# Two products with one weight block in one 512-column matmul, summed when PSUM is read

## The chip, the cores and the metric

The kernel runs on one core of one Trainium2 chip. The metric is the device time of one execution in microseconds (us); three executions of the kernel before were timed. TensorE (PE in the profile, PEld for its weight loads) multiplies, VectorE (DVE) and ScalarE (ACT) do the elementwise work, GpSimd (POOL) sets constants, and SyncE (SP) issues all the large DMAs.

## The reference

Two layers of a diffusion backbone on 256 latent tokens and 256 context tokens of width 1024, in float32:

```python
x = x + 0.5 * m[2] * swiglu(modulate(x, norm_g[l, 0], m[0], m[1]), ffn1_wi[l], ffn1_wo[l])
# even layer: window attention with sink | bidirectional gated linear attention
y = jnp.concatenate([o_a, gla_output(o_b, rb, gla_g)], axis=-1) @ w_out
# odd layer: multi-scale pooling mixer
# then, in both, a second half-step SwiGLU
def swiglu(h, wi, wo):
    a, u = jnp.split(h @ wi, 2, axis=-1)
    return (jax.nn.silu(a) * u) @ wo
```

D_FF is 2816, so a down projection (`@ wo`) contracts 22 blocks of 128 into 8 blocks of 128 output columns; the mixer's output (`@ w_out`) contracts 8 blocks into 8. The context stream is needed only up to the first layer's mixer. The output is the latent stream after a last RMSNorm.

## The kernel before, in words

Activations lie with the features on partitions and the 256 tokens along the free dimension. A product keeps float32 precision by three matmuls: both operands are split into a high part (rounded to the type fp32r) and a low part (what rounding left), and high times high, high times low and low times high are summed in PSUM. The weights of a product come in by DMA as `raw`; ACT rounds them to `hi` (L142) and DVE subtracts to get `lo` (L143), in `weight` (L136). Each of `raw`, `hi` and `lo` has four buffers.

The program has these stages, with their place in the profiled span:

- the first SwiGLU for both streams (to 402 us), whose down projection runs twice with 512 columns, that is with both streams side by side;
- the mixer of the even layer (402 to 569 us), whose pieces of work are ordered by a planner (`Flow`, L61) with costs written by hand; its output projection is `output` (L925), in four groups of two output blocks (`OUT_N`), contraction blocks in the order `OUT_K`;
- the second SwiGLU, one stream (569 to 760 us, called ffn1 below), the third (760 to 950, ffn2), the pooling mixer (950 to 972) and the fourth (972 to the end, ffn3).

A SwiGLU stage (`ffn`, L337) first makes 22 pairs of up products (`product`, L303: 258 columns, of which 256 are tokens and two carry the shift); silu and the multiplication give a block of G, which `parts` (L328) splits into `G[0]` (ACT, L329) and `G[1]` (DVE, L330), two tiles. Then, for each of 8 output blocks n, 22 contraction blocks times three matmuls (L418 to L420) fill one PSUM bank, 256 columns wide for one stream. One DVE instruction (L430, called the eviction here) multiplies the bank by the gate and adds it to the residual stream, and `nxt.block` prepares the next stage's operand: a scaled copy by ACT (L299), its low part by DVE (L300), a square by ACT (L273) and a sum by DVE (L274). `Final.block` (L1083) does the like for the last norm.

DVE also makes the modulation vectors, 1024 elements at a time (L172, "dots" below), in a number per output block set by `RATES0` to `RATES3`: 1.2 in ffn1, 2 in ffn2, none in ffn3. Their weights (`rawm`, two buffers) share SP's queue with the stage's own weights. The order of each engine's instructions is fixed when the program is built, by a scheduler with its own estimates; engines then wait for one another by semaphores, each in its own order.

The mixer's output has the same three matmuls (L935 to L937) on the tile O, `[128, 2, 8, 258]`, whose second dimension is the part, and the same eviction (L951), two after each group.

Of the kernel before, what the change touches and what calls it, by code (L numbers as in the profile page):

```python
# [16 lines left out]
T = 256  # L17
# [43 lines left out]
class Flow:  # L61
    """Orders pieces of work so that TensorE always has one whose operands are there.

    A piece is a generator that emits instructions and yields step(...) with the time that they
    take on TensorE, what the other engines then do one after the other, the events that the
    next step needs and those that this one sets."""
# [34 lines left out]
def step(pe=0.0, post=(), needs=(), sets=()):  # L101
    return pe, post, needs, sets


class Body:
# [57 lines left out]
    def mod_dot(self, w, l, ch, k, s):  # L163
        """One block of adaLN's columns: a row of w_mod per partition times silu(c), plus its bias.
        Chunks 2 and 8 gate a half step and are halved here."""
# [19 lines left out]
    def step_mod(self, dots):  # L185
        """Spends `dots` of VectorE's time on the modulation and loads ahead for the next step."""
        self.credit += dots
        while self.units and self.credit >= len(self.units[0][3]):
            self.credit -= self.next_unit()
        while len(self.loaded) < min(2, len(self.units)):  # L190
            self.loaded.append(self.mod_load(*self.units[len(self.loaded)][:3]))
# [38 lines left out]
    def rstd_tables(self, sss, pool, tag, spare=None):  # L230
        """1/rms by the scalar engine's Ln and Exp and one Newton step, all streams at once."""
# [22 lines left out]
    def token_stats(self, ss):  # L254
        """Mean squares with the tokens on partitions, for rsqrt on a few columns."""
# [55 lines left out]

    def narrow(self, ps, w, X):
        """Product with 32 columns: a quarter of the contraction on each 32 columns of the array, and so
        four partial sums on 128 partitions."""
# [8 lines left out]
    def swiglu(self, out, za, zu, ba, bu):  # L323
        """out = silu(za + ba) (zu + bu); za is overwritten."""
        self.silu = self.nc.scalar.activation(za, za, AF.Silu, bias=ba)  # L325
        self.nc.vector.scalar_tensor_tensor(out=out, in0=zu, scalar=bu, in1=za, op0=ALU.add, op1=ALU.mult)  # L326

    def parts(self, G, j, c, src):  # L328
        self.nc.scalar.copy(G[0][:, j, c], src)  # L329
        return self.nc.vector.tensor_tensor(G[1][:, j, c], src, G[0].bitcast(F32)[:, j, c], op=ALU.subtract)  # L330

# [5 lines left out]
    def ffn(self, l, wi, wo, Xs, rstds, gate, streams, nxt, rates, first=None):  # L337
        """x += 0.5 gate swiglu(modulated x); with `first`, the first stream goes ahead alone in the
        first half, without the shift, and the second stream's operand brings both streams' shifts."""
# [8 lines left out]
        for h in range(nh):  # L348
            G = None if first is not None and h == 0 else [self.t(gp, [128, pph, W], F32R, f"g{i}") for i in range(2)]
            split = first is not None and h == 0  # L350
            if split:
# [18 lines left out]
                G = [self.t(gp, [128, pph, W], F32R, f"g{i}") for i in range(2)]  # L370
# [37 lines left out]
            for n in range(KB):  # L408
# [4 lines left out]
                for (k0, nk), (hi, lo) in zip(parts, ws):  # L413
                    for q in range(nk):
# [3 lines left out]
                        nc.tensor.matmul(ps[:, :W], hi[:, c], G[0][:, kk, :], start=(kk == 0), stop=False)  # L418
                        nc.tensor.matmul(ps[:, :W], hi[:, c], G[1][:, kk, :], start=False, stop=False)  # L419
                        nc.tensor.matmul(ps[:, :W], lo[:, c], G[0][:, kk, :], start=False, stop=(kk == pph - 1))  # L420
# [7 lines left out]
                for i in range(ns):  # L428
                    xk = self.xs[streams[i]][:, n, :]
                    nc.vector.scalar_tensor_tensor(out=xk, in0=ps[:, i * T:(i + 1) * T],  # L430
# [12 lines left out]
    def run(self):  # L443
# [39 lines left out]
        # the scale of the first norm comes first, and block by block the operand that waits for it  # L483
# [19 lines left out]
        def parts(X, xa, k):  # L503
            """Operand blocks k and k + 1 from the scaled blocks."""
# [8 lines left out]
        def begin(early):  # L513
            """First pairs, one block of the contraction after the other as the scale arrives."""
# [23 lines left out]
        def during(p):  # L538
            """Second stream's operand, between the pairs of the first pass."""
# [76 lines left out]
    def mixer(self, cur, nxt):  # L616
# [5 lines left out]
        # lp: until the end of the mixer; zp: projections; gp: gates, then sp: attention and states  # L622
# [31 lines left out]
        # ---- projections  # L654
# [77 lines left out]
        # ---- gates of one direction and two heads  # L732
# [76 lines left out]
        def attend(j, g, qb, u):  # L809
            """Scores, softmax and transposed probabilities of 128 queries of a head; the second  # L810
            half then brings the head's values."""
# [43 lines left out]
        def states(d, b):  # L855
            order = (0, 1, 2, 3) if d == 0 else (3, 2, 1, 0)

            def outer(ps, lhsT, tb, start, stop):
                """Keys times values of two heads, a head on each half of the array's columns."""
# [64 lines left out]
        # ---- output projection  # L924
        def output():  # L925
# [5 lines left out]
            def part(n, w, ps, ks):  # L931
                hi, lo = w
                for k in ks:
                    c = slice(k * 128, (k + 1) * 128)
                    nc.tensor.matmul(ps[:, :T], hi[:, c], O[:, 0, k, :T], start=(k == order[0]), stop=False)  # L935
# [266 lines left out]
```

## Time and profile before

| | us |
|---|---|
| median of three runs | 1172.83 (1171.46 to 1173.13) |
| span of the profiled execution, first to last instruction | 1168.3 |
| median less span | 4.5 |
| PE busy | 1150.8 (99%) |
| DVE busy | 945.2 (81%) |
| ACT busy | 564.2 (48%) |

The page gives no time for the profiled execution other than its span; the 4.5 us is taken for what lies around it. Busy time counts a matmul from its start to its modelled end, and matmuls overlap, so the distance between the starts of neighbours says more than the length of one. Granted clock 1.00 is TensorE's upper level, 2.4 GHz.

### The profile page before, as it was taken

How to read it: one execution, taken by the hardware profiler on the slowest of the kernel's cores; microseconds unless marked ns; L12 is line 12 of the kernel's file. 1: busy time of each engine (PE TensorE's matmuls, PEld its weight loads, DVE VectorE, ACT ScalarE, POOL GpSimd, SP SyncE). 2: the span in 40 equal slices, each digit the busy share in tenths (PEclk: the TensorE clock that was granted, in tenths of full speed). 3: DMA queues.
4: the chain of work that ended last, by engine and by line, in shares of the span. 5: the costliest groups of instructions: out<-in, count | busy, mean ns of one | idle time of the engine just before them, and what ended most of it. 6: DMA issues, size and time to landing. Idle time of an engine off the chain costs nothing.

```text
span 1168.3 us, 22254 instructions
## 1 busy us (share of the span) xinstructions
PE 1150.8 (99%) x8778; PEld 1098.1 (94%) x8778; DVE 945.2 (81%) x1708; ACT 564.2 (48%) x935; POOL 10.0 (1%) x32
## 2 busy tenths in 40 slices
PE   7999999999999999999999999999999999999997
PEld 5999988999998899787999999999999999999997
DVE  6898888998888889766998867799886888777553
ACT  4647532232244464565565544545554455445442
POOL 0000000000000200000000000000000000000000
PEclk9999999999999999999999999999999999999999
DMA  9866557667766535311777757888786964555562
GB/s 341 294 257 221 163 178 241 239 222 254 253 187 208 186 123 175 113 70 54 269 255 255 259 182 254 270 279 298 263 267 193 312 235 146 181 181 176 152 182 87
DMA packets 74555, 247.60 MB, mean 212 GB/s; under 512 B 8273, under 2 KB 8913, under 8 KB 74194
## 3 DMA queue, kind: packets, MB, share of 16 engines
q1 hardware_dynamic: 74450, 246.17, 63.0%
q8 instruction: 69, 1.13, 0.4%
q14 instruction: 36, 0.29, 0.1%
HBM read 245.09 MB, written 1.05 MB: 211 GB/s over the span
## 4 chain that ended last, share of the span: by engine, by line
PE 90%; DVE 5%; DMA 3%; ACT 1%; issue 1%; SPq 0%; DVEq 0%; ACTq 0%
PE t_mm L309 18%; PE t_mm L308 18%; PE t_mm L310 18%; PE t_mm L418 9%; PE t_mm L419 9%; PE t_mm L420 9%; PE t_mm L522 2%; PE t_mm L842 1%; PE t_mm L815 1%; DVE t_junk L172 1%; DVE t_lo L143 1%; PE t_mm L935 1%; PE t_mm L832 1%; DMA t_raw<-wi0k 1%; PE t_mm L936 1%
## 5 line engine op out<-in xcount | busy, mean ns | idle before, releaser
L308 PE MATMUL t_mm<-t_xA,t_hi 128*128 128x258 f32 (+1 forms) x1888 | 537.8, 285 | 1.3 <-DVE t_x L868 1.3
L309 PE MATMUL t_mm<-t_xA,t_hi 128*128 128x258 f32 (+1 forms) x1888 | 533.6, 283 | 0.3 <-DVE t_xA L300 0.3
L310 PE MATMUL t_mm<-t_xA,t_lo 128*128 128x258 f32 (+1 forms) x1888 | 532.7, 282 | 1.1 <-DVE t_lo L143 1.1
L142 ACT CAST t_hi<-t_raw 128x1024 fp32r<-128x1024 f32 (+1 forms) x344 | 326.5, 950 | 363.9 <-PE t_mm L309 184.8
L143 DVE TENSOR_TENSOR t_lo<-t_raw,t_hi 128x1024 fp32r<-128x1024 f32 (+1 forms) x344 | 377.5, 1099 | 79.0 <-ACT t_hi L142 77.9
L309 PEld LDWEIGHTS t_mm<-t_xA,t_hi 128*128 128x128 f32 x1888 | 357.7, 189 | 2.4 <-issue 1.4
L308 PEld LDWEIGHTS t_mm<-t_xA,t_hi 128*128 128x128 f32 x1888 | 355.8, 189 | 3.9 <-DVE t_x L868 1.5
L310 PEld LDWEIGHTS t_mm<-t_xA,t_lo 128*128 128x128 f32 x1888 | 357.2, 189 | 1.5 <-DVE t_lo L143 1.5
L418 PE MATMUL t_mm<-t_g,t_hi 128*128 128x256 f32 (+1 forms) x704 | 218.0, 310 | 0.0
L420 PE MATMUL t_mm<-t_g,t_lo 128*128 128x256 f32 (+1 forms) x704 | 217.3, 309 | 0.0
L419 PE MATMUL t_mm<-t_g,t_hi 128*128 128x256 f32 (+1 forms) x704 | 217.1, 308 | 0.0
L172 DVE CUSTOM_DVE_ANT_0 t_junk<-t_rawm,t_x 128x1024 bf16<-128x1024 f32 x142 | 181.9, 1281 | 19.3 <-DMA t_rawm<-wmod 18.5
L419 PEld LDWEIGHTS t_mm<-t_g,t_hi 128*128 128x128 f32 x704 | 132.7, 188 | 6.8
L420 PEld LDWEIGHTS t_mm<-t_g,t_lo 128*128 128x128 f32 x704 | 132.4, 188 | 6.8
L418 PEld LDWEIGHTS t_mm<-t_g,t_hi 128*128 128x128 f32 x704 | 132.3, 188 | 6.8
L325 ACT ACTIVATE t_za<-t_za 128x256 f32<-128x256 f32 x99 | 49.8, 508 | 48.3 <-DVE t_za L334 48.1
L329 ACT CAST t_g<-t_za 128x256 fp32r<-128x256 f32 x88 | 35.5, 406 | 68.9 <-DVE t_za L326 63.7
L334 DVE TENSOR_TENSOR t_zu<-t_mm,t_rstd 128x257 f32<-128x257 f32 x66 | 28.1, 426 | 30.8 <-PE t_mm L310 30.7
L326 DVE SCALAR_TENSOR_TENSOR t_za<-t_zu,t_za 128x256 f32<-128x256 f32 x88 | 42.2, 484 | 6.9 <-ACT t_za L325 0.6
L172 DVE CUSTOM_DVE_ANT_0 t_junk<-t_w,t_x 128x1024 bf16<-128x1024 f32 x32 | 41.0, 1282 | 5.4 <-DMA t_w<-wmod 5.2
L330 DVE TENSOR_TENSOR t_g<-t_za,t_g 128x256 fp32r<-128x256 f32 x88 | 36.7, 420 | 3.9 <-ACT t_g L329 3.8
L334 DVE TENSOR_TENSOR t_za<-t_mm,t_rstd 128x257 f32<-128x257 f32 x66 | 27.7, 424 | 10.6 <-PE t_mm L310 10.4
(220 smaller groups left out, 858.0 us busy)
## 6 DMA issues: line engine op xcount, KB each, us to landing
t_raw<-wi SPq DMA_DIRECT2D x190, 512.0 KB, 4.4
t_rawm<-wmod SPq DMA_DIRECT2D x118, 512.0 KB, 4.5
t_raw<-wo SPq DMA_DIRECT2D x64, 384.0 KB, 3.1
t_raw<-wo SPq DMA_DIRECT2D x64, 320.0 KB, 3.2
t_raw<-win SPq DMA_DIRECT2D x18, 512.0 KB, 3.4
t_w<-wmod SPq DMA_DIRECT2D x16, 512.0 KB, 7.0
t_raw<-wmod SPq DMA_DIRECT2D x10, 512.0 KB, 4.6
t_raw<-wi0k SPq DMA_DIRECT2D x8, 512.0 KB, 6.8
```

The source lines that it names most:

```text
L142: nc.scalar.copy(hi[:, :n], raw[:, :n])
L143: self.mark = nc.vector.tensor_tensor(lo[:, :n], raw[:, :n], hi.bitcast(F32)[:, :n], op=ALU.subtract)
L172: self.nc.vector.tensor_tensor_reduce(out=junk, in0=w, in1=self.srow[s], scale=0.5 if half else 1.0, scalar=b, op0=ALU.mult, op1=ALU.add, ...
L308: nc.tensor.matmul(ps[:, :n], hi[:, c], X[:, 0, k, :n], start=(k == 0), stop=False)
L309: nc.tensor.matmul(ps[:, :n], hi[:, c], X[:, 1, k, :n], start=False, stop=False)
L310: nc.tensor.matmul(ps[:, :n], lo[:, c], X[:, 0, k, :n], start=False, stop=(k == KB - 1))
L325: self.silu = self.nc.scalar.activation(za, za, AF.Silu, bias=ba)
L326: self.nc.vector.scalar_tensor_tensor(out=out, in0=zu, scalar=bu, in1=za, op0=ALU.add, op1=ALU.mult)
L334: self.nc.vector.tensor_tensor(z[:, :n], ps[:, :n], r[:, :n], op=ALU.mult)
L418: nc.tensor.matmul(ps[:, :W], hi[:, c], G[0][:, kk, :], start=(kk == 0), stop=False)
L419: nc.tensor.matmul(ps[:, :W], hi[:, c], G[1][:, kk, :], start=False, stop=False)
L420: nc.tensor.matmul(ps[:, :W], lo[:, c], G[0][:, kk, :], start=False, stop=(kk == pph - 1))
```

## The change

G becomes one tile `[128, 2, blocks, columns]`. For a single stream, `merged` replaces three matmuls by two: `hi` times both parts of the operand, side by side, in one matmul of 512 columns (columns 0 to 255 the product with the high part, 256 to 511 the product with the low part), and `lo` times the high part, added into columns 256 to 511. The bank then holds two sums, and `residual` adds both to the stream with two dependent instructions. This is done in the down projections of ffn1, ffn2 and ffn3 and in the mixer's output. The first SwiGLU's down projection keeps its three matmuls of 512 columns and reads the new G.

```diff
+    def merged(self, ps, hi, lo, X, first, last):
+        nc = self.nc
+        nc.tensor.matmul(ps, hi, X, start=first, stop=False)
+        nc.tensor.matmul(ps[:, T:], lo, X[:, 0], start=False, stop=last)
+
+    def residual(self, xk, ps, gate):
+        for q in (0, 1):
+            self.nc.vector.scalar_tensor_tensor(out=xk, in0=ps[:, q * T:(q + 1) * T], scalar=gate, in1=xk,
+                                                op0=ALU.mult, op1=ALU.add)
...
     def parts(self, G, j, c, src):
-        self.nc.scalar.copy(G[0][:, j, c], src)
-        return self.nc.vector.tensor_tensor(G[1][:, j, c], src, G[0].bitcast(F32)[:, j, c], op=ALU.subtract)
+        self.nc.scalar.copy(G[:, 0, j, c], src)
+        return self.nc.vector.tensor_tensor(G[:, 1, j, c], src, G.bitcast(F32)[:, 0, j, c], op=ALU.subtract)
...
-                        nc.tensor.matmul(ps[:, :W], hi[:, c], G[0][:, kk, :], start=(kk == 0), stop=False)
-                        nc.tensor.matmul(ps[:, :W], hi[:, c], G[1][:, kk, :], start=False, stop=False)
-                        nc.tensor.matmul(ps[:, :W], lo[:, c], G[0][:, kk, :], start=False, stop=(kk == pph - 1))
+                        if ns == 1:
+                            self.merged(ps, hi[:, c], lo[:, c], G[:, :, kk, :], kk == 0, kk == pph - 1)
+                            continue
+                        nc.tensor.matmul(ps, hi[:, c], G[:, 0, kk, :], start=(kk == 0), stop=False)
+                        nc.tensor.matmul(ps, hi[:, c], G[:, 1, kk, :], start=False, stop=False)
+                        nc.tensor.matmul(ps, lo[:, c], G[:, 0, kk, :], start=False, stop=(kk == pph - 1))
...
+                    if ns == 1:
+                        self.residual(xk, ps, self.mod_tile(l, gate, 0)[:, n:n + 1])
+                        nxt.block(0, xk, n)
+                        continue
...
-                    nc.tensor.matmul(ps[:, :T], hi[:, c], O[:, 0, k, :T], start=(k == order[0]), stop=False)
-                    nc.tensor.matmul(ps[:, :T], hi[:, c], O[:, 1, k, :T], start=False, stop=False)
-                    nc.tensor.matmul(ps[:, :T], lo[:, c], O[:, 0, k, :T], start=False, stop=(k == order[-1]))
+                    self.merged(ps, hi[:, c], lo[:, c], O[:, :, k, :T], k == order[0], k == order[-1])
...
-                    nc.vector.scalar_tensor_tensor(out=xk, in0=ps[:, :T], scalar=gate[:, n:n + 1], in1=xk,
-                                                   op0=ALU.mult, op1=ALU.add)
+                    self.residual(xk, ps, gate[:, n:n + 1])
```

The rest of the diff takes out comments.

## Rows read from the trace of the kernel before

**Rows 1.** The page: what PE waited for, by line, all waits of the span (us in total, times, longest).

```profile
PE t_mm L522 <- DMA t_raw<-wi0k: 4.8, 1, 4.8
...
PE t_mm L309 <- DVE t_xA L300: 0.3, 1, 0.3
```

**Rows 2.** Busy time by stretch (us from the span's start, busy us and instructions of each engine, granted clock, DMA share, GB/s): the mixer's output, then the down projections of ffn1, ffn2 and ffn3.

```profile
551.00:569.00 18.00, 18.00 (x152) 18.00 (x152) 14.74 (x26) 11.21 (x21) 0.00 (x0) 1.00 0.79 266
...
700.00:760.00 60.00, 60.00 (x503) 60.00 (x502) 45.70 (x70) 29.66 (x45) 0.00 (x0) 1.00 0.81 262
...
886.00:950.00 64.00, 64.00 (x536) 64.00 (x535) 52.88 (x84) 31.34 (x47) 0.00 (x0) 1.00 0.81 271
...
1096.00:1158.50 62.50, 62.50 (x525) 62.50 (x524) 33.05 (x50) 25.92 (x42) 0.00 (x0) 1.00 0.50 145
```

**Rows 3.** Groups of PE instructions by form: the three matmuls' first line in the down projections of one stream and in the mixer's output (count, busy us, mean ns).

```profile
L418 PE MATMUL t_mm<-t_g,t_hi 128*128 128x256 f32 x528 | 149.5, 283 | 0.0
...
L935 PE MATMUL t_mm<-t_xA,t_hi 128*128 128x256 f32 x64 | 18.6, 295 | 0.0
```

**Rows 4.** Timeline of PE in ffn1's down projection (start us, length us): the first and the last of 19 matmuls that follow each other, 18 distances.

```profile
719.80 0.28 PE L419 MATMUL t_mm<-t_g,t_hi 128*128 128x256 f32 x1
...
721.96 0.28 PE L419 MATMUL t_mm<-t_g,t_hi 128*128 128x256 f32 x1
```

**Rows 5.** Timeline of PE in the first SwiGLU's down projection: the first and the last of 15 matmuls, 14 distances.

```profile
159.66 0.39 PE L419 MATMUL t_mm<-t_g,t_hi 128*128 128x512 f32 x1
...
162.83 0.39 PE L418 MATMUL t_mm<-t_g,t_hi 128*128 128x512 f32 x1
```

**Rows 6.** Timeline in ffn1's up products: the first and the last of 13 matmuls, 12 distances.

```profile
639.87 0.28 PE L309 MATMUL t_mm<-t_xA,t_hi 128*128 128x258 f32 x1
...
641.30 0.28 PE L309 MATMUL t_mm<-t_xA,t_hi 128*128 128x258 f32 x1
```

**Rows 7.** Timeline of DVE in the mixer's output: the evictions of the last two groups (in brackets the idle time before, and what ended it), and the low parts of the next operand that follow the last.

```profile
562.97 0.88 DVE L951 SCALAR_TENSOR_TENSOR t_x<-t_mm,t_x 128x256 f32<-128x256 f32 x2 [0.85 <-PE t_mm L937]
...
568.71 0.88 DVE L951 SCALAR_TENSOR_TENSOR t_x<-t_mm,t_x 128x256 f32<-128x256 f32 x2 [0.95 <-PE t_mm L937]
...
570.80 0.48 DVE L300 SCALAR_TENSOR_TENSOR t_xA<-t_x,t_xA 128x256 fp32r<-128x256 f32 x1
...
571.54 0.48 DVE L300 SCALAR_TENSOR_TENSOR t_xA<-t_x,t_xA 128x256 fp32r<-128x256 f32 x1
```

**Rows 8.** Timeline of PE at the start of ffn1: matmuls that read the low parts of the operand's last two blocks.

```profile
571.34 0.39 PE L309 MATMUL t_mm<-t_xA,t_hi 128*128 128x258 f32 x1
...
572.41 0.29 PE L309 MATMUL t_mm<-t_xA,t_hi 128*128 128x258 f32 x1
```

**Rows 9.** Timeline of DVE in the mixer: two dependent instructions on 256 columns, one after the other.

```profile
547.46 0.42 DVE L917 TENSOR_TENSOR t_osq<-t_oy 128x256 f32<-128x256 f32 x1 [0.36 <-ACT t_oy L915]
547.91 0.42 DVE L918 SCALAR_TENSOR_TENSOR t_osq<-t_osq,t_ov 128x256 f32<-128x256 f32 x1
```

**Rows 10.** Timeline at the end of ffn1: DVE from the last dot but one to the low part of the operand's last block, then PE's matmul that waits for it.

```profile
759.46 1.28 DVE L172 CUSTOM_DVE_ANT_0 t_junk<-t_rawm,t_x 128x1024 bf16<-128x1024 f32 x1 [0.66 <-DMA t_rawm<-wmod]
...
760.67 0.48 DVE L430 SCALAR_TENSOR_TENSOR t_x<-t_mm,t_x 128x256 f32<-128x256 f32 x1
...
762.74 0.39 PE L309 MATMUL t_mm<-t_xA,t_hi 128*128 128x258 f32 x1 [0.29 <-DVE t_xA L300]
```

**Rows 11.** Timeline at the end of ffn2: DVE's last eviction, and PE's matmuls before and after its wait for the last sum of squares (L274).

```profile
951.14 0.48 DVE L430 SCALAR_TENSOR_TENSOR t_x<-t_mm,t_x 128x256 f32<-128x256 f32 x1
...
953.35 0.28 PE L1004 MATMUL t_mm<-t_lo,t_xA 128*128 128x256 f32 x1
953.77 0.61 PE L258 MATMUL t_mm<-t_x,t_ss 128*128 128x2 f32 x4
```

**Rows 12.** Timeline at the end of ffn3, all engines: the last eviction and the square that waits for it.

```profile
1159.35 0.48 DVE L430 SCALAR_TENSOR_TENSOR t_x<-t_mm,t_x 128x256 f32<-128x256 f32 x1 [6.06 <-PE t_mm L420]
...
1159.93 0.42 ACT L1089 ACTIVATE t_sq<-t_x 128x256 f32<-128x256 f32 x1
```

**Rows 13.** Timeline of DVE and PE in the mixer's first output group: the low part of O's last block, and three matmuls of L935 that PE ran before the first of L936.

```profile
551.62 0.42 DVE L805 TENSOR_TENSOR t_xA<-t_oy,t_xA 128x256 fp32r<-128x256 f32 x1
...
551.23 0.58 PE L935 MATMUL t_mm<-t_xA,t_hi 128*128 128x256 f32 x3
551.64 0.28 PE L936 MATMUL t_mm<-t_xA,t_hi 128*128 128x256 f32 x1
```

**Rows 14.** Timeline of DVE in ffn2's down projection: one output block from eviction to eviction, those of its rows before which DVE was idle (in brackets, us).

```profile
934.96 0.48 DVE L430 SCALAR_TENSOR_TENSOR t_x<-t_mm,t_x 128x256 f32<-128x256 f32 x1
935.60 0.82 DVE L143 TENSOR_TENSOR t_lo<-t_raw,t_hi 128x640 fp32r<-128x640 f32 x1 [0.15 <-ACT t_hi L142]
...
941.87 0.96 DVE L143 TENSOR_TENSOR t_lo<-t_raw,t_hi 128x768 fp32r<-128x768 f32 x1 [0.69 <-ACT t_hi L142]
942.88 0.48 DVE L430 SCALAR_TENSOR_TENSOR t_x<-t_mm,t_x 128x256 f32<-128x256 f32 x1
```

**Rows 15.** DMA queues between 894 and 942 us, in ffn2's down projection (packets, MB, share of 16 engines).

```profile
q1 hardware_dynamic: 4960, 14.29, 88.1%
```

**Rows 16.** Groups of DVE instructions by form: 512 columns that lie in two runs of 256 (L507), and in one run (L744).

```profile
L507 DVE TENSOR_TENSOR t_xA<-t_x,t_xA 128x512 fp32r<-128x512 f32 x8 | 5.5, 692 | 2.0 <-ACT t_xA L506 1.9
...
L744 DVE TENSOR_TENSOR t_gm<-t_gm,t_ge 128x512 f32<-128x512 f32 x4 | 2.7, 685 | 0.0
```

More of the change, by code (lines that the diff above doesn't have):

```diff
@@ L348, in ffn @@
         for h in range(nh):
-            G = None if first is not None and h == 0 else [self.t(gp, [128, pph, W], F32R, f"g{i}") for i in range(2)]
+            G = None if first is not None and h == 0 else self.t(gp, [128, 2, pph, W], F32R, "g")
             split = first is not None and h == 0
@@ L369, in ffn @@
                 self.modpool = gp
-                G = [self.t(gp, [128, pph, W], F32R, f"g{i}") for i in range(2)]
+                G = self.t(gp, [128, 2, pph, W], F32R, "g")
             for j in range(pph):
```

## The prediction

> **What bounds the kernel now.** I read the waits of PE first, because the page has PE busy for 99% of the span. In the whole span PE waits for little, and within the stages the change touches only for DVE at the end of ffn1, 0.3 us [rows 1]. The stretches say the same: in the mixer's output and in the three down projections PE is busy for all of the time at a granted clock of 1.00, the upper level of 2.4 GHz, while DVE is busy for 53 to 83% and DMA for at most 81% [rows 2]. So PE's own pace sets these stages, and the question is what one matmul costs there. That is the distance between starts, not the length: 2.16 us over 18 distances, 120.0 ns, for 256 columns [rows 4], and 3.17 us over 14, 226.4 ns, for 512 columns in the first SwiGLU's down projection [rows 5]. Twice the columns cost 1.89 times as much. At 2.4 GHz 256 columns are 106.7 ns and 512 are 213.3, so either form carries about 13 ns that does not grow with the columns. That is what a merged matmul can save; the number of columns that pass through PE stays at 768 per block.
>
> **The change part by part.**
>
> *Matmuls.* A contraction block now costs 3 x 120.0 = 360.0 ns, afterwards 226.4 + 120.0 = 346.4 ns, 13.6 ns less. There are 528 such blocks (3 stages x 8 x 22), the count of L418's 256-column form [rows 3]: 7.2 us. In the mixer's output two evictions are 5.74 us apart for 48 matmuls [rows 7], 119.6 ns each, so the 64 blocks [rows 3] save 12.8 ns each: 0.8 us. All of it lies on PE, which has no idle time to absorb it: 8.0 us.
>
> What no row shows is a moving operand of two runs: all matmuls of the trace read their columns in one. From below, the merged matmul costs what the contiguous one does, 226.4 ns; from above, two matmuls' pace, 240 ns and over, if the second run starts like a new instruction. The nearest row is on another engine: DVE takes 692 ns for 512 columns in two runs and 685 in one [rows 16], 1% more. I take 226.4.
>
> *The second eviction.* 32 more DVE instructions. Each depends on the first; dependent instructions of 256 columns start 0.45 us apart [rows 9]. Within a stage they are beside PE's work. DVE in ffn2, the fullest: from eviction to eviction 7.92 us, of which 0.15 + 0.69 idle [rows 14]; 7.08 + 0.45 = 7.53 us against PE's new 22 x 346.4 ns = 7.62 us. It fits by 0.09 us, and the 0.15 us of idle right behind the eviction is where the new instruction lands. The lo blocks and dots behind it on DVE slip by up to 0.45 us; the four buffers hold all four weight parts of an output block, so they are made most of a block before PE needs them. DMA at 88.1% [rows 15] goes to 88.1 x 7.92/7.62 = 91.6%. I cost the middle of the stages at nothing; without that cover it is the first rival.
>
> *The ends of stages*, where PE waits for the last block:
>
> - ffn1: the last eviction starts at 760.67 behind a dot whose weights came late, and PE, which already waits for the low part of the last block, starts L309 at 762.74 [rows 10]. 0.45 us later: 0.45 lost.
> - ffn2: PE's statistics matmul starts 0.42 us after its predecessor instead of 0.12, waiting for the sum behind the eviction of 951.14 [rows 11]: another 0.45.
> - ffn3: the square follows the eviction directly [rows 12], and all that comes after is a chain to the end: 0.45.
> - Mixer: the last group has two evictions, hence 0.9 us more before the low parts that follow. The first of them ends at 570.80 + 0.48 = 571.28 [rows 7], and its reader starts at 571.34; the second ends at 572.02 against 572.41 [rows 8]. So PE loses 0.8 us if its order stays, about 0.4 if the scheduler puts the second up product ahead. I take 0.6.
>
> *The mixer's first group.* PE ran three L935 while the low part of O's last block was still being made, and L936 then came on time [rows 13]. A merged matmul needs both parts, so this head start, 3 x 0.12 us, is gone: 0.4 us, if nothing else can be put there.
>
> *The mixer's other groups.* DVE is now 5.74 - 0.95 = 4.79 us per group [rows 7], with two more evictions 5.69, against PE's 16 x 346 ns = 5.54. Three groups of 0.15 us are 0.45 at worst, nothing if the buffers cover it: 0.2.
>
> *G as one tile.* Same bytes. In the first SwiGLU, G is written again for the second half when its last reader is done; G[1] now waits for L420 instead of L419, one distance of 0.23 us [rows 5], behind DVE work that comes after ACT's copy anyway: nothing.
>
> *The sum.* 8.0 - 3 x 0.45 - 0.6 - 0.4 - 0.2 = 5.45 us. The span of 1168.3 becomes 1162.9; the median of the runs lies 4.5 us above the profiled span, which I leave as it is: **1167.4 us**, 0.47% less.
>
> **The rivals.** About 0.2%, 2.3 us, is what a measurement of this kernel can tell from no change.
>
> 1. *ffn2 does not speed up*, because DVE (7.53 of 7.62 us) or DMA (91.6%) becomes its bound. For it: any wait of 0.1 us per block that DVE cannot make up. Against: the lead of most of a block, and that in ffn1 with 1.2 dots and ffn3 with none DVE has more room. ffn2's 2.4 us would be gone: 1169.8.
> 2. *The second run costs*, and the change ends slower. The place is the second half of each merged matmul, the price whatever is over 226.4 ns, times 592. At 240 ns the matmuls save nothing and the 2.55 us of ends and waits remain: 1175.4. From there on it is slower than can be told from no change; between 232 and 240 ns the saving is 4.7 to 0 us, and it is within it. Against: two runs cost DVE 1% [rows 16], and 1% of 226 ns is 2 ns, or 1.3 us in all.
> 3. *Little of the 13 ns goes with the instruction.* Rows 4 and 5 differ in stage as well as in columns, so part of the excess could belong to what surrounds it. If a merged matmul saved 2.6 ns, 592 of them save 1.5 us against 2.55: 1173.9. The Trainium skill speaks for this: "TensorE: Matmul & The Clock Gate", section "Back-to-back issue gap", gives a fixed part of 2.5 ns per matmul beside the columns, by which a pair of 256 becomes one of 512 for 2.6 ns less (an estimate from its formula, 109.2 x 2 - 215.8). The trace does not agree: 13.3 and 13.1 ns above the columns in two places [rows 4, 5].
> 4. *The short matmul gets faster too.* 258 columns take 1.43 us over 12 distances, 119.2 ns [rows 6], no more than 256 take [rows 4]. So columns may not set the pace there, but the weight load; behind a long matmul the next weights are ready early. At the 512 form's 0.442 ns per column the short one would be 113.2 ns: 592 x 6.8 ns = 4.0 us more, 1163.4. Against: the load for the long one still has only a short matmul to hide behind.
>
> That the change doesn't do what it says I leave out: the diff has no condition that could skip it.
>
> **How the numbers follow.** Forecast 0.67 (its own range 1165.8 to 1168.8, from the mixer's terms and the order the scheduler finds); rival 1 0.13, of which a third within the bound; rival 2 0.11, of which 0.07 slower and 0.04 within; rival 3 0.03; rival 4 0.06. Faster: 0.67 + 0.09 + 0.06 = 0.82. Within: 0.04 + 0.04 + 0.03 = 0.11. Slower: 0.07. The range, 1163.8 to 1171.0, holds the forecast, rival 1, most of rival 4 and the cheap side of rival 2, and leaves out some 0.15.
>
> **What would show it.** L418's successor with 512 columns should start 226 ns before its short partner and 346 ns before its own like; evictions in ffn2 should be 7.62 us apart, two DVE instructions each, with DVE idle for less than 0.2 us per block; PE's waits should show 0.7 us at ffn1's end and a wait at ffn1's start. A distance of 235 ns or more for the merged matmul makes it wrong (rival 2); so does 7.9 us between evictions in ffn2 (rival 1). A wait of several us that no row here announces, from another order of instructions, would be a case I have not priced.

## The result: 0.5% less time

The changed kernel takes 1166.2 us (median of 4 runs, 1164.3 to 1166.6) against 1172.35 for the kernel before beside it (4 runs, 1171.5 to 1173.1): a ratio of 0.9949, 95% interval 0.9935 to 0.9963. The forecast was 1167.4. The profiled execution has a span of 1164.5 us and a time of 1166.5.

By the page PE is busy for 98% of the span and DVE for 82%. What PE waited for in the changed kernel (us in total, times, longest):

```profile
PE t_mm L1122 <- ACT t_sq L1107: 1.3, 1, 1.3
...
PE t_mm L258 <- DVE t_ss L274: 0.6, 1, 0.6
```

The wait for a low part at the end of ffn1 [rows 1] is no longer among the large ones; the sum of squares at the end of ffn2 (L258) and the square at the very end (L1122) are.

Next the stretches of the four changed stages, from the first to the last start of their merged matmuls (L317; columns as in [rows 2]): ffn1, ffn2, ffn3, the mixer's output.

```profile
697.10:758.40 61.30, 61.30 (x353) 53.47 (x352) 50.12 (x80) 31.92 (x47) 0.17 (x2) 1.00 0.80 256
885.90:947.20 61.30, 61.30 (x353) 53.57 (x352) 55.08 (x91) 31.96 (x47) 0.00 (x0) 1.00 0.83 282
1091.90:1154.60 62.70, 62.70 (x364) 54.83 (x363) 36.85 (x59) 27.55 (x43) 0.00 (x0) 1.00 0.52 150
530.00:569.20 39.20, 39.20 (x229) 31.40 (x227) 28.47 (x73) 21.16 (x47) 0.00 (x0) 1.00 0.33 120
```

PE is still busy for all of each, at a granted clock of 1.00 (the 2.4 GHz level). From the start of a stage's first matmul to that of its last, short ones included, the four (in the same order) take 61.5, 61.5, 62.9 and 39.4 us, and in the kernel before 63.2, 63.2, 64.5 and 39.7. So the stages shrink by 1.7, 1.7, 1.6 and 0.3: 5.3 us. The gaps, counted from a stage's last matmul, grow where the prediction said they would: from ffn2 to the pooling products (L1028, now L1046) 10.1 to 10.5 us, from ffn3 to the end of the span 9.3 to 9.7. That leaves 4.5 us which stages and gaps explain.

The forms and the pace. The first view is the group of the merged matmuls (answers to [rows 3]); the second is PE's timeline in ffn1, one pair and the start of the next, then the first and the last of 21 consecutive merged matmuls, 20 distances (answers to [rows 4]).

```profile
L317 PE MATMUL t_mm<-t_g,t_hi 128*128 128x512 f32 x528 | 185.9, 394 | 0.0
```

```profile
718.47 0.39 PE L317 MATMUL t_mm<-t_g,t_hi 128*128 128x512 f32 x1
...
719.52 0.39 PE L317 MATMUL t_mm<-t_g,t_hi 128*128 128x512 f32 x1
719.75 0.28 PE L318 MATMUL t_mm<-t_g,t_lo 128*128 128x256 f32 x1
719.87 0.39 PE L317 MATMUL t_mm<-t_g,t_hi 128*128 128x512 f32 x1
...
725.47 0.39 PE L317 MATMUL t_mm<-t_g,t_hi 128*128 128x512 f32 x1
```

7.00 us over 20 is 350.0 ns per contraction block, where 360 were before and 346.4 were predicted. Within the pair the next start is 0.23 us after a merged matmul and 0.12 after a short one; the averages from the unrounded starts are 232 and 118 ns. The merged matmul is 6 ns slower than the 226.4 of [rows 5], the short one 2 ns faster than 120.0. For all 528, 528 x 10.0 ns = 5.3 us instead of 7.2; the three stages shrink by 5.0.

The ends. DVE at the end of ffn1, from the last block's first eviction to the low part, and PE around the same time (answers to [rows 10]):

```profile
759.64 0.48 DVE L323 SCALAR_TENSOR_TENSOR t_x<-t_mm,t_x 128x256 f32<-128x256 f32 x1
760.03 1.27 DVE L172 CUSTOM_DVE_ANT_0 t_junk<-t_rawm,t_x 128x1024 bf16<-128x1024 f32 x1
...
761.24 0.48 DVE L323 SCALAR_TENSOR_TENSOR t_x<-t_mm,t_x 128x256 f32<-128x256 f32 x1
...
762.77 0.48 DVE L300 SCALAR_TENSOR_TENSOR t_xA<-t_x,t_xA 128x256 fp32r<-128x256 f32 x1
```

```profile
762.06 0.28 PE L309 MATMUL t_mm<-t_xA,t_hi 128*128 128x258 f32 x1
762.31 0.39 PE L308 MATMUL t_mm<-t_xA,t_hi 128*128 128x258 f32 x1
```

The scheduler has put a dot between the two evictions, so the low part starts 4.4 us after PE's last merged matmul. PE hardly notices: between 762.06 and 762.31 it loses 0.13 us, because the new order gives it other products first. In the kernel before, the matmul ahead of the waiting one of [rows 10] started 0.57 us before it (762.17 and 762.74), a loss of 0.45:

```profile
762.17 0.28 PE L308 MATMUL t_mm<-t_xA,t_hi 128*128 128x258 f32 x1
```

ffn2's end (answers to [rows 11]) and ffn3's end (answers to [rows 12]) went as foreseen:

```profile
948.13 0.48 DVE L323 SCALAR_TENSOR_TENSOR t_x<-t_mm,t_x 128x256 f32<-128x256 f32 x1
```

```profile
951.14 0.58 PE L258 MATMUL t_mm<-t_x,t_ss 128*128 128x2 f32 x4 [0.59 <-DVE t_ss L274]
```

```profile
1155.16 1.00 DVE L323 SCALAR_TENSOR_TENSOR t_x<-t_mm,t_x 128x256 f32<-128x256 f32 x2 [5.60 <-PE t_mm L318]
...
1156.26 0.42 ACT L1107 ACTIVATE t_sq<-t_x 128x256 f32<-128x256 f32 x1 [0.51 <-DVE t_x L323]
...
1156.73 0.38 PE L1122 MATMUL t_mm<-t_x,t_sq 128*128 128x2 f32 x2 [1.27 <-ACT t_sq L1107]
```

From the eviction's start to the square 1.10 us pass, 0.58 before [rows 12].

### The profile page after: what moved, and what is told of

Its sections match the earlier page's. It is cut to its first block, busy times and chain, and to the rows that moved or that the text cites. A ratio compares the mean times of both kernels' runs of the same rounds, so it can differ in the third digit from the quotient of the medians.

```text
span 1164.5 us, 21097 instructions
## 1 busy us (share of the span) xinstructions
PE 1146.9 (98%) x8186; PEld 1067.0 (92%) x8186; DVE 955.7 (82%) x1740; ACT 566.6 (49%) x935; POOL 10.0 (1%) x32
## 4 chain that ended last, share of the span: by engine, by line
PE 83%; DVE 9%; DMA 4%; issue 2%; ACT 1%; SPq 0%; DVEq 0%; ACTq 0%
PE t_mm L308 15%; PE t_mm L310 15%; PE t_mm L309 15%; PE t_mm L317 12%; PE t_mm L318 6%; PE t_mm L436 3%; PE t_mm L435 3%; PE t_mm L437 3%; DVE t_junk L172 3%; DMA t_rawm<-wmod 3%; PE t_mm L543 3%; DVE t_lo L143 2%; PE t_mm L863 1%; PE t_mm L836 1%; ACT t_hi L142 1%
## 5 line engine op out<-in xcount | busy, mean ns | idle before, releaser
L317 PE MATMUL t_mm<-t_g,t_hi 128*128 128x512 f32 x528 | 185.9, 394 | 0.0
L318 PE MATMUL t_mm<-t_g,t_lo 128*128 128x256 f32 x528 | 147.4, 279 | 0.0
L317 PEld LDWEIGHTS t_mm<-t_g,t_hi 128*128 128x128 f32 x528 | 99.0, 187 | 23.2
L318 PEld LDWEIGHTS t_mm<-t_g,t_lo 128*128 128x128 f32 x528 | 99.0, 188 | 0.0
L435 PE MATMUL t_mm<-t_g,t_hi 128*128 128x512 f32 x176 | 68.5, 389 | 0.0
L436 PE MATMUL t_mm<-t_g,t_hi 128*128 128x512 f32 x176 | 68.5, 389 | 0.0
L437 PE MATMUL t_mm<-t_g,t_lo 128*128 128x512 f32 x176 | 68.5, 389 | 0.0
```

The costliest lines, as they stand in the source:

```text
L317: nc.tensor.matmul(ps, hi, X, start=first, stop=False)
L318: nc.tensor.matmul(ps[:, T:], lo, X[:, 0], start=False, stop=last)
L435: nc.tensor.matmul(ps, hi[:, c], G[:, 0, kk, :], start=(kk == 0), stop=False)
L436: nc.tensor.matmul(ps, hi[:, c], G[:, 1, kk, :], start=False, stop=False)
L437: nc.tensor.matmul(ps, lo[:, c], G[:, 0, kk, :], start=False, stop=(kk == pph - 1))
```

## The experiments

Stages and gaps are cut as above, from matmul to matmul. "Output block" is the distance between the first matmuls of two output blocks, 22 contraction blocks: 7.92 us before, 7.70 in the changed kernel (22 x 350.0 ns). Intervals are 95% intervals of the ratio to the kernel before.

### The changed kernel again

No edit.

> The changed kernel again, as the yardstick of this chip. A merged matmul and its short partner together 350.0 ns in the down projections and 356 ns in the mixer's output, as in the changed kernel's first trace; 5 to 7 us less than the kernel before.

1165.6 us (1165.1 to 1166.8, 5 runs) against 1171.7 (1170.0 to 1173.4, 9 runs): 0.9950 (0.9938 to 0.9963). Output blocks of 7.70 us, spans of stages as above to 0.1 us. The size holds. In each run the time is 1.8 to 2.0 us above that run's own span; the spans of the nine runs of the kernel before reach from 1168.2 to 1171.6.

### Is it the second run of the operand?

G and the mixer's O lie with the two parts of a block side by side, so a merged matmul reads one run of 512.

```diff
-self.t(gp, [128, 2, pph, W], F32R, "g")
+self.t(gp, [128, pph, 2, W], F32R, "g")
...
-nc.tensor.matmul(ps, hi, X, start=first, stop=False)
+nc.tensor.matmul(ps, hi, X.rearrange("p x t -> p (x t)"), start=first, stop=False)
```

> G and O laid out so that the two parts of a block are neighbours, and the merged matmul reads 512 columns in one run. Theory A (the second run is what costs): the pair takes 226.4 + 120.0 = 346 ns in all four places, that is 528 x 3.6 + 64 x 10 ns = 2.5 us less than the changed kernel. Theory B (a long matmul beside a short one costs 3.6 ns more, whatever the layout): the pair stays at 350 ns in the down projections; the mixer's comes to 350 as well if only its rows of 258 were to blame.

1165.35 us, 0.9949 (0.9936 to 0.9961). PE's timeline in ffn1, the first and the last of 21 merged matmuls:

```profile
718.54 0.39 PE L317 MATMUL t_mm<-t_g,t_hi 128*128 128x512 f32 x1
...
725.54 0.39 PE L317 MATMUL t_mm<-t_g,t_hi 128*128 128x512 f32 x1
```

Again 7.00 us, 350.0 ns. Two runs cost a merged matmul nothing that can be seen; only the mixer's output is 0.1 us shorter (39.3).

A second run changed the layout by stage: parts side by side but still read with two dimensions in ffn1, as changed in ffn2, rows 258 apart in ffn3, rows 256 apart in the mixer.

> Four layouts in one kernel, read by the pace of the pair in each stage. ffn1: parts adjacent, but the matmul's operand still written with two dimensions. ffn2: as changed, two runs of 256 with 22528 bytes between their starts. ffn3: two runs in rows of 258. Mixer's output: two runs in rows of 256. Theory A: ffn1 346, ffn2 350, ffn3 and mixer 350 if only the number of runs counts; ffn3 356 and mixer 350 if the rows of 258 (starts off a round address) cost on top. Theory B: 350 in all four, or 356 in ffn3.

1165.05 us (one run). 7.70, 7.70, and 7.98 instead of 7.94 in ffn3 (its blocks also hold the turns of the last norm), the mixer 39.3. In ffn3 the build also starts G elsewhere (179,712 instead of 180,064), so that the two are not parted there. No layout brings back the 3.6 ns.

### What do the second evictions cost?

The second instruction of `residual` is left out, so the product of the operand's low part with the weights' high part and that of its high part with the weights' low part are not added to the stream.

```diff
-        for q in (0, 1):
+        for q in (0,):
```

> The changed kernel with only the first of the two instructions at eviction; the sum in columns 256 to 511, that is high times low and low times high of these four products, is left out of the output. Theory: the second instruction costs only at the ends of stages, 0.45 us each in ffn1, ffn2 and ffn3 and up to 0.9 in the mixer: 1.2 to 2.2 us less than the changed kernel, and evictions in ffn2 stay 7.70 us apart. Rival (DVE sets the pace in ffn2): over 3 us less, evictions in ffn2 closer than 7.70 us.

1165.1 us, 0.9942 (0.9926 to 0.9958). The output block stays at 7.70. What changes is the end: PE's wait for the last square falls from 1.27 to 0.75 us.

```profile
1155.17 0.38 PE L1122 MATMUL t_mm<-t_x,t_sq 128*128 128x2 f32 x2 [0.75 <-ACT t_sq L1107]
```

The gap after ffn3 is 9.3 instead of 9.7; the stages and gaps from the mixer to the pooling products differ from the changed kernel's by 0.1 us at most. By the time it is some 0.5 us in all, less than the 1.2 to 2.2 expected and not clear of the scatter, since the intervals overlap. So 32 more instructions on DVE cost what the last of them costs, and hardly more.

The other direction: a third instruction of the same size at each of these evictions, into a tile that nobody reads.

```diff
+        extra = self.t(self.cp, [128, T], F32, "extra", 1)
+        self.nc.vector.scalar_tensor_tensor(out=extra, in0=ps[:, T:], scalar=gate, in1=xk,
+                                            op0=ALU.mult, op1=ALU.add)
```

> The changed kernel with a third DVE instruction of the same size at each eviction, which writes a scratch tile that nothing reads. Theory (in mid-stage DVE's room hides evictions until it runs out): ffn1 and ffn3 keep their pace of 7.70 us from eviction to eviction; in ffn2 DVE needs 7.53 + 0.45 = 7.98 us for 7.70, and the stage grows by at most 7 x 0.28 = 2.0 us, less if the lead of the weight parts takes it; mixer 0.9 us per group on DVE, 16 x 356 ns = 5.70 against 6.6, so 2 to 3 us longer. In all 2 to 5 us over the changed kernel. Rival (DVE is far from any bound): under 1 us.

1171.0 us (1169.0 to 1175.1), 0.9997 (0.9983 to 1.0011): all of the gain is gone. But not where one would look for it. The output blocks stay at 7.70 us in ffn1 and ffn2; the mixer's output grows by 2.1 us to 41.6, and the gap behind ffn2 by 2.9, from 10.5 to 13.4. Of PE's waits in this kernel one lies in that gap:

```profile
PE t_mm L258 <- DVE t_ss L274: 1.9, 1, 1.9
```

DVE's timeline in ffn2, evictions of one block after the other and the one row with a long wait:

```profile
917.05 0.48 DVE L323 SCALAR_TENSOR_TENSOR t_x<-t_mm,t_x 128x256 f32<-128x256 f32 x1
918.92 0.82 DVE L143 TENSOR_TENSOR t_lo<-t_raw,t_hi 128x640 fp32r<-128x640 f32 x1 [1.39 <-ACT t_hi L142]
...
926.07 0.48 DVE L323 SCALAR_TENSOR_TENSOR t_x<-t_mm,t_x 128x256 f32<-128x256 f32 x1
...
933.60 0.48 DVE L323 SCALAR_TENSOR_TENSOR t_x<-t_mm,t_x 128x256 f32<-128x256 f32 x1
```

The instruction fits: from 926.07 on the blocks follow every 7.53 us without idle, less than PE's 7.70. What hurts is where things stand. The scheduler now puts a low part between the evictions, and at 918.92 it waits 1.39 us for its high part with the second eviction queued behind it. DVE is then over a microsecond late, regains at most 0.17 per block, and the last block's evictions start at 949.09, 0.96 after the changed kernel's; with the third instruction also ahead of it, the last sum starts 1.4 us later (951.95 instead of 950.57). PE never stalls within the eight blocks, since its weights are made so far ahead; the delay comes due at the end of the stage, where PE waits 1.9 us for that sum instead of 0.6.

These 1.3 us are less than half of the gap's 2.9. The rest is TensorE's clock. Behind the wait it falls to its lower level, 1.2 GHz; first a stretch of this kernel, then the changed kernel from the statistics matmul to the pooling products, which take 6.8 us there and 8.3 here (columns as in [rows 2]):

```profile
953.00:956.40 3.40, 3.40 (x17) 3.40 (x18) 2.85 (x12) 0.46 (x1) 0.00 (x0) 0.50 0.30 95
951.14:957.94 6.80, 6.80 (x44) 6.29 (x45) 4.98 (x15) 2.68 (x3) 0.00 (x0) 1.00 0.49 167
```

In the mixer the scheduler has put two up products of ffn1 among the output's matmuls, and PE waits first for the high part of their weights, then for a low part of the output's:

```profile
561.14 0.39 PE L308 MATMUL t_mm<-t_xA,t_hi 128*128 128x258 f32 x1 [1.06 <-ACT t_hi L142]
...
562.07 0.39 PE L318 MATMUL t_mm<-t_xA,t_lo 128*128 128x256 f32 x1 [0.42 <-DVE t_lo L143]
```

Between the two merged matmuls around these rows 2.6 us pass instead of 0.35, about what the mixer's output grows by.

### Is it the alternation of hi and lo?

All merged matmuls of a weight part first, then all short ones; in the mixer two merged and two short.

```diff
-                            self.merged(ps, hi[:, c], lo[:, c], G[:, :, kk, :], kk == 0, kk == pph - 1)
+                        for w in (hi, lo):
+                            for q in range(nk):
...
+                                    nc.tensor.matmul(ps, w[:, c], G[:, :, kk, :], start=(kk == 0), stop=False)
...
+                                    nc.tensor.matmul(ps[:, T:], w[:, c], G[:, 0, kk, :], start=False, stop=(kk == pph - 1))
```

> The changed kernel with its matmuls in another order: in a down projection all merged matmuls of a weight part (5 or 6 blocks) first, then its short ones; in the mixer's output the two merged ones of a group's pair of output blocks, then the two short ones. Theory B (a change between 512 and 256 columns costs 3.3 ns per pair): with one change per part instead of per block, 226.7 + 120.0 + 3.3/5.5 = 347.3 ns per block, so a down projection is 176 x 2.7 = 0.5 us shorter, 1.4 us in all. Rival (the 3.3 ns belong to a 256-column matmul or a 512-column one on a bank that both write): 350 ns per block in any order, no change in time.

1168.9 us, 0.9973 (0.9962 to 0.9984): slower than the changed kernel. PE's timeline in ffn2, where consecutive matmuls of a line stand in one row; from the first of these rows to the last 11 merged and 11 short ones start:

```profile
900.49 1.33 PE L433 MATMUL t_mm<-t_g,t_hi 128*128 128x512 f32 x5
901.66 0.76 PE L435 MATMUL t_mm<-t_g,t_lo 128*128 128x256 f32 x5
902.26 1.55 PE L433 MATMUL t_mm<-t_g,t_hi 128*128 128x512 f32 x6
903.65 0.88 PE L435 MATMUL t_mm<-t_g,t_lo 128*128 128x256 f32 x6
904.38 1.33 PE L433 MATMUL t_mm<-t_g,t_hi 128*128 128x512 f32 x5
```

3.89 us over 11 blocks, 353.6 ns. Merged behind merged starts after 233 ns on average, short behind short after 120: grouping does not bring the merged one back to 226.4, and the short one is back at the pace of [rows 4]. Besides, DVE's order is another one, here too with a low part between the two evictions of a block, and the gap behind ffn2 grows to 13.2 us, with a longer wait and, behind it, the lower clock:

```profile
PE t_mm L258 <- DVE t_ss L274: 1.8, 1, 1.8
...
955.20:958.60 3.40, 3.40 (x18) 3.40 (x17) 1.99 (x9) 0.03 (x1) 0.00 (x0) 0.50 0.41 151
```

Two more runs put the parts side by side as well, in groups as long as the weight part (6 or 5 contraction blocks) and in groups of two:

```diff
+                        for q0 in range(0, nk, 6):
+                            for x, w in enumerate((hi, lo)):
+                                for q in range(q0, min(q0 + 6, nk)):
```

> The contiguous layout of e1 together with the order of e4 in the down projections (all merged matmuls of a weight part, then its short ones); the mixer's output as in e1. In e4 a merged matmul behind a merged one took 232.9 ns and a short behind a short 120.7, with operands in two runs. Theory C (two runs cost 6 ns, and apart from that a change of length costs 3.3 ns per pair, so that e1 and e4 each removed one of the two): merged behind merged 226.7, short behind short 120.0, 347.3 ns per block, a down projection 0.5 us shorter than the changed kernel's 61.3. Rival D (the 6 ns go with something else that the first SwiGLU has not, as that each matmul has another weight block, while there two in three share one): merged behind merged stays at 233 and the stage at 62.0 us.

1171.5 us, 0.9995 (0.9982 to 1.0008). Output blocks of 7.77 us, as rival D has it; the gap from ffn1 to ffn2 130.9 (127.3 as changed), behind ffn2 15.6, with a wait of 2.6 us for the sum and the clock at 0.50 for 6.8 us behind it (955.8 to 962.6).

> As e7, with groups of two blocks: two merged, two short. Theory C: half as many changes of length as in e1, so 346.7 + 1.7 = 348.4 ns per block, a down projection 0.3 us shorter than 61.3. Rival D: between e1's 350 and e4's 353 ns per block, 61.3 to 62.0 us.

1166.5 us, 0.9961 (0.9946 to 0.9976). 7.73 us. With one run, with groups and with both, a merged matmul does not come down to the pace of the same shape in the first SwiGLU.

### Is it where G begins?

In the first SwiGLU the build places G at a multiple of 512 bytes per partition (125,440). In the one-stream stages it begins at 171,872 or 180,064, a multiple of 32 only. Here G is padded so that it begins at 171,520 or 179,712, multiples of 512. ffn1 keeps the changed kernel's layout and order, ffn2 is grouped with one run, ffn3 has one run in the changed order.

```diff
+                G = self.t(gp, [128, 2 * pph * W + 88], F32R, "g")[:, :2 * pph * W]
```

> One thing the first SwiGLU's down projection has and the others have not: its G begins at a byte address (per partition) that is a multiple of 512, theirs at one that is 32 above a multiple of 64 (171872 and 180064). Here G of ffn1, ffn2 and ffn3 begins at a multiple of 512. ffn1: two runs and the order as changed; ffn2: one run and the order of e7 (all merged of a weight part, then its short ones); ffn3: one run, order as changed; mixer's output as in e1. Theory E (the start address costs the 6 ns): merged behind merged 226.7 and short behind short 120.0 in ffn2, and a pair near 346.7 ns in ffn1 and ffn3, down projections of 60.7 to 61.0 us. Rival F (something else, as the sequence of weight blocks): 350, 353 and 350 ns per block as before, 61.3 and 62.0 us.

1167.2 us (one run). In ffn1, the first and the last of 21 merged matmuls:

```profile
718.34 0.39 PE L444 MATMUL t_mm<-t_g,t_hi 128*128 128x512 f32 x1
...
725.27 0.39 PE L444 MATMUL t_mm<-t_g,t_hi 128*128 128x512 f32 x1
```

6.93 us, 346.5 ns: the predicted pace to the nanosecond, which looked like the cause found. But ffn2 came at 7.71 us per block, and there merged behind merged still took 232 ns; and ffn3 had blocks of 7.85 us beside blocks of 8.00. So the last two runs put the aligned start alone into the changed kernel, in all three stages, and into the kernel before.

> The changed kernel with one edit: the buffer of the intermediate of the three one-stream stages is a little larger, so that the build places its start at a multiple of 512 bytes per partition (171,520, 171,520 and 179,712 instead of 171,872, 171,872 and 180,064); layout in two runs and order of the matmuls as changed. Theory E (the start address costs 3.3 ns per contraction block, and the order of the weights' parts has nothing to do with it): an output block of 22 contraction blocks every 7.63 us in the first and second one-stream feed-forward (changed: 7.70), 7.87 in the third (7.94), so that 3 x 22 x 8 x 3.3 ns = 1.7 us go from PE's work; VectorE, at 7.6 us per block by its work in the second, is then the bound there or close to it, and may give 0.3 us back at the end of that stage. Time 1163.9, 0.9935 of the kernel before (0.9920 to 0.9945). Rival F (what the run before showed came from the layout in one part with the adjacent runs, not from the address): 7.70 in all three, and the time of the changed kernel, 1165.6, ratio 0.995.

1166.3 us (1165.1 to 1168.3), 0.9960 (0.9946 to 0.9973). In ffn1:

```profile
718.47 0.40 PE L317 MATMUL t_mm<-t_g,t_hi 128*128 128x512 f32 x1
...
725.54 0.40 PE L317 MATMUL t_mm<-t_g,t_hi 128*128 128x512 f32 x1
```

7.07 us, 353.5 ns: slower, not faster; 7.77 us per output block in ffn1 and ffn2. Neither theory named this. The theory of the start address falls, at least as it was put: the 352 matmuls of ffn1 are the same in this kernel and in the one before it, with the same addresses of operand, weights and PSUM bank, and took 346.5 ns per block there and 353.5 here.

ffn3 shows both paces within one stage. Its output blocks are 7.76, 7.91, 7.85, 7.85, 8.00, 8.00 and 7.85 us apart, and the run before has the same seven numbers, on another chip and with G in one run instead of two. PE's timeline around one change, 19 distances before it and 19 behind it:

```profile
1117.08 0.39 PE L317 MATMUL t_mm<-t_g,t_hi 128*128 128x512 f32 x1
...
1123.66 0.39 PE L317 MATMUL t_mm<-t_g,t_hi 128*128 128x512 f32 x1
...
1124.01 0.38 PE L1143 MATMUL t_mm<-t_x 128*128 128x128 f32 x2
...
1124.93 0.40 PE L317 MATMUL t_mm<-t_g,t_hi 128*128 128x512 f32 x1
...
1131.65 0.40 PE L317 MATMUL t_mm<-t_g,t_hi 128*128 128x512 f32 x1
```

6.58 us are 346.3 ns per contraction block, 6.72 are 353.7. In both runs the pace of ffn3 changes only where the two small matmuls of the last norm (L1143) stand between two output blocks, at four of their six places; from a block's third pair to its last it holds. The granted clock (1.00) and, as the build places them, G and the weights' buffers are the same on both sides; only the PSUM bank is another in each block, and in ffn1 all eight banks had one pace. So neither chip, layout, start address nor bank decides by itself between the two paces; what does was not found.

This run helps with the grouped order too. Its blocks are as slow as those of the first grouped kernel, yet its gap behind ffn2 is 10.5 us, as in the changed kernel. So the 353 ns need no grouping. What grouping added in that gap is 2.7 us: DVE's order, by 1.2 us of longer wait, and the lower clock behind the wait. The run before parts these two: its ffn2 is grouped as well, PE waits 2.5 us for the sum, but the clock stays at 1.00, and the gap is 12.5 us; with 2.6 us of wait and 6.8 us at the lower clock it was 15.6. Why the clock fell in one and not in the other stays open.

> The kernel before with its two intermediate buffers of the one-stream stages in one larger buffer, which starts at a multiple of 512 bytes per partition (171,520 and 194,048 instead of 171,872 and 194,400); nothing else changed. Theory E1 (the address costs a 512-column matmul with an operand in two runs only): an output block stays at 7.92 us, 120.0 ns per matmul of 256 columns, and the time of the kernel before. Theory E2 (the address costs every matmul a little): 7.85 us per block, some 119 ns per matmul as in the mixer's output, and about 1.7 us less than before.

1171.9 us (one run; the kernel before beside it 1170.95). PE's timeline, 18 distances in 2.16 us as in [rows 4]:

```profile
718.42 0.28 PE L423 MATMUL t_mm<-t_g,t_hi 128*128 128x256 f32 x1
...
720.58 0.28 PE L423 MATMUL t_mm<-t_g,t_hi 128*128 128x256 f32 x1
```

120.0 ns, as theory E1 has it: a stage of 256-column matmuls keeps its pace with G at either start.

### A second profile of the kernel before

> The kernel before, for a second profile: its first profiled span, 1168.3 us, lies at the low end of what other executions show. If this one is longer, the stage where it is longer tells whether the changed stages or others scatter. Theory: the down projections and the mixer's output take the same 63.0 and 39.5 us from their first to last block, and the scatter is in the first 130 us, where PE waits for DMA.

1174.6 us, span 1172.8, 4.5 more than the profile of [rows 2]. The four stages are as long as there to 0.1 us. The difference lies elsewhere: the first down projection starts at 154.1 us instead of 149.9, and the gap from ffn1 to ffn2 is 128.6 instead of 127.7. PE's longest wait for DMA, where the scatter was expected, is the same (4.7 and 4.8 us). But at 83.87 us PE has waited 1.6 us for a low part of the weights (0.9 in the first profile), and behind that the clock falls. The same stretch in this profile and in the first; the number behind PE's busy time counts its matmuls:

```profile
84.60:88.00 3.40, 3.40 (x19) 3.40 (x18) 3.40 (x5) 1.05 (x1) 0.00 (x0) 0.50 0.97 358
84.60:88.00 3.40, 3.40 (x31) 3.40 (x30) 3.40 (x5) 0.82 (x2) 0.00 (x0) 1.00 1.02 407
```

## Why the prediction was right, and where it was not

**PE's pace is the bound, and a fixed part goes with the instruction: right.** Of the 13.6 ns per block 10.0 went. The term "matmuls" was too large by 528 x 3.6 ns = 1.9 us. It took the pace of 512 columns from another stage and that of 256 from a row of 256s, and assumed that the two would add up when they alternate. The merged one took 232 ns, not far from the 235 that would have spoken against the prediction by its own sign. Layout, order and start address were each tried; none explains it, and it stays open.

**Rival 3, that little of the 13 ns goes with the instruction: wrong.** By the formula that the Trainium skill, "TensorE: Matmul & The Clock Gate", section "Back-to-back issue gap", gives for an isolated matmul, 2.6 ns would have gone per block (an estimate). The trace shows 10.0.

**Rival 2, that the second run costs: wrong in its cause, close in its size.** One run of 512 has the same 350.0 ns. But the merged matmul came at 232 ns, 5.6 above the 226.4, and there this rival's "within" begins. That the change is still clearly faster is in part luck: the short matmul gained 2 ns, and the ends cost less than priced.

**Rival 4, that the short matmul gets faster too: mostly wrong.** It starts the next one after 118 ns instead of 120.0, not 113.2.

**Rival 1, that ffn2 does not speed up: wrong, and by more than its margin.** DVE in ffn2 from one block's evictions to the next, the rows with idle time before them (answers to [rows 14]), and the DMA queue in the stretch of [rows 15]:

```profile
932.33 1.00 DVE L323 SCALAR_TENSOR_TENSOR t_x<-t_mm,t_x 128x256 f32<-128x256 f32 x2
...
939.08 0.96 DVE L143 TENSOR_TENSOR t_lo<-t_raw,t_hi 128x768 fp32r<-128x768 f32 x1 [0.26 <-ACT t_hi L142]
940.03 1.00 DVE L323 SCALAR_TENSOR_TENSOR t_x<-t_mm,t_x 128x256 f32<-128x256 f32 x2
```

```profile
q1 hardware_dynamic: 5038, 14.71, 88.4%
```

Evictions are 7.70 us apart, with 0.26 us of idle shown. The kernel with the third instruction does its block in 7.53 us without idle, so two need some 7.1 (7.53 less the 0.40 by which such instructions follow each other there): 0.6 us of room, where the prediction found 0.09 by counting as work whatever was not marked idle. DMA rose to 88.4%, not to 91.6. What the prediction had right is the reason why no middle of a stage would stall, the lead of the weights.

**The ends and waits: 2.55 us predicted, about 0.9 found.** ffn2's and ffn3's ends cost 0.4 each by the gaps, about as priced. The step that failed is "0.45 us later: 0.45 lost" at ffn1's end. It took PE's order as given, and the scheduler found another: 0.13 us lost where 0.45 had been, and the gap to ffn2 did not grow (127.7 to 127.3, and 127.8 in the changed kernel's second profile). The mixer's end was priced at 0.6; from its last matmul to ffn1's first down matmul 127.55 became 127.68. Its output was to gain 0.8 and lose 0.4 + 0.2, 0.2 net; it gained 0.3, with pairs of 354 to 358 ns from group to group (the last three groups) where 346 were priced. The head start of the first group is hardly missed. From another head's values, which PE makes just ahead of the group's end, to the group's first eviction 4.16 us pass before (548.89 to 553.05) and 4.30 now (549.77 to 554.07), 0.1 more instead of 0.4.

**What lies around the span: wrong.** The prediction added 4.5 us, the median of three runs less the span of one profile. In every run the time is 1.7 to 2.2 us above the span of the same execution; the rest of the 4.5 was that the profiled execution was one of the shortest of its kernel. That the forecast came within 1.2 us of the measured time is partly luck: the span is 1.6 us longer than the 1162.9 predicted, and the 4.5 was 2.5 too much. In the sum of 5.45 too, two errors partly cancelled: too much taken off by the matmuls (8.0 instead of the 5.3 by which the stages shrink), too much put on by ends and waits. By the stages and gaps 4.5 us are explained; the medians differ by 6. The other 1.6 us are not located. Parts that the change does not touch scatter by as much: the start of the first down projection (149.9 to 154.1 us in three profiles with the old matmuls) and the gap from ffn1 to ffn2 (127.7, 128.6 and 128.6 there; 127.1 to 127.8 in seven with the new ones in the changed order). From the start of the first down projection to the end of the span, 1018.4, 1018.7 and 1019.3 us pass with the old matmuls and 1014.0 and 1014.2 in the two profiles of the changed kernel, 4.2 to 5.3 less.

## What to carry to other kernels

Where PE's pace is the bound and matmuls have 256 columns, two that share their weights can become one of 512, with the sums parted at the eviction; that took 10 of 360 ns per contraction block here, and the operand need not be contiguous. When an engine beside the bound gets more work, look at its order and at the end of the stage: a pace that stays the same does not show that the engine keeps up, and a new order can cost more than the instruction. Look at the granted clock behind every long wait of TensorE: in three of these kernels, and in one of two profiles of the kernel before, a wait of 1.6 to 2.6 us was followed by 3.4 or 6.8 us at the lower clock, which cost some 1.5 or 3 us more. Read the time around the span from one execution, never as the median less another execution's span.

## What was not expected of the hardware

The pace of alternating 512- and 256-column matmuls is not fixed by their shapes: 346.5, 350.0 and 353.5 ns per block were seen with the same instructions on operands of the same layout. With G where the changed kernel has it, 350.0 came out in ffn1 and ffn2 of every kernel in the changed order, whatever the layout; with G at a multiple of 512 it was 346.5 in one kernel's ffn1 and 353.5 in another's, with identical addresses, and both in ffn3 of either kernel, block by block in the same places on two chips. What the other engines do beside PE was not varied. Matmuls of 512 columns alone (226 to 227 ns in the first SwiGLU) and of 256 alone (120.0) show nothing of the kind.
